# Up projection: weight rests formed by accumulating transfers, every second chunk rounded by a casting transfer

## Chip, cores and metric

The kernel runs on one core of a Trainium2 chip. The metric is device time in microseconds (us) for one execution. Before the change the median of two runs is 957.73 us (957.66 to 957.80).

## What is computed

The reference is one layer of a streaming encoder: a token mixer (pooling, latent attention and spatial gating, merged and projected), then a gated MLP with a causal convolution of three taps over positions. Sequence 512, model width 1024, MLP width 2816. The change lies in the MLP's up projection:

```python
def _conv_ffn(h, w_up, conv_w, conv_b, w_down):
    z = h @ w_up                      # (512 x 1024) @ (1024 x 5632)
    zp = jnp.pad(z, ((0, 0), (CONV_W - 1, 0), (0, 0)))
    zc = conv_b + conv_w[0] * zp[:, 0:S]
    for k in range(1, CONV_W):
        zc = zc + conv_w[k] * zp[:, k:k + S]
    val, gate = jnp.split(zc, 2, axis=-1)
    return (jax.nn.silu(gate) * val) @ w_down
```

All of it is float32.

## The kernel before

TensorE multiplies in the type fp32r, which holds fewer digits than float32. So each float32 operand is split: `hi` is the operand rounded to fp32r, `lo` is the rest, operand minus `hi`, again as fp32r. A product is then the sum of three: hi times lo, lo times hi, hi times hi.

The up projection's weight is laid out as 44 chunks `wup[m]` of 128 partitions x 1024 floats (512 KB). A chunk holds the weights of 128 output channels: eight blocks of 128 x 128, one for each block `k` of the model width. Chunks come in pairs: 2i is the value half and 2i+1 the gate half of the same 128 channels. The activations `h2_hi[k]`, `h2_lo[k]` (128 x 512) stay in SBUF through the stage. Chunks 0 to 5 are split earlier (`early_split`, `early_low`) and multiplied in two halves of 256 positions while the second half of `h2` is still made; chunks 6 to 43 (38 chunks, 19 pairs) go through `wsplit`, and these the change touches.

For one such chunk, before:

- `load` (lines 82 to 86): SP's queue issues a transfer from HBM to a tile `wup` (tag "raw", three buffers).
- L92: ScalarE rounds it to `wuph` (tag "whi", two buffers).
- L93: VectorE subtracts: `wupl` = `wup` - `wuph` (tag "wlo", two buffers).
- `mm_chunk` (lines 110 to 116): TensorE runs 24 matmuls of 512 columns into one PSUM bank `pzu`: sixteen with `wuph` (L113, L114), then eight with `wupl` (L116).
- L1384, L1387, L1391: ScalarE and twice VectorE make the convolution's three taps from `pzu`.

After each pair ScalarE takes Silu of the gate half (L1401), POOL multiplies the halves (L1402), ScalarE and VectorE split the product (L1405, L1406) for the down projection. In every second one of the first sixteen pairs, SP also loads two tiles `adar` of 256 KB (L848) for a later modulation row, which VectorE adds up (L850, L852). Near the end of the stage POOL scales the first down projection chunks (L1098).

The order on each engine's queue is written by the framework when the kernel is built; it follows the dependencies and its own estimate of times. On the chip each engine works its queue in that order, and an instruction that waits holds up those behind it. A buffer is written again only when its last reader is done. There are eight PSUM banks, so products of several chunks may be open at once.

Of the kernel before, what the change touches and what calls it, by code (L numbers as in the profile page):

```python
# [9 lines left out]
F32R = mybir.dt.float32r  # L10
I32 = mybir.dt.int32
AF = mybir.ActivationFunctionType
ALU = mybir.AluOpType
AX = mybir.AxisListType

P = 128
S = 512
D = 1024
# [32 lines left out]
def trunk(ctx: ExitStack, tc: tile.TileContext, A, out):  # L51
    nc = tc.nc
# [4 lines left out]
    wp = ctx.enter_context(tc.tile_pool(name="wp", bufs=2))  # L57
# [3 lines left out]
    def ps(name):  # L61
        return pp.tile([P, 512], F32, name=name, tag="ps")
# [16 lines left out]
    def f(ap):  # L79
        return ap.bitcast(F32)  # L80

    def load(src, n, name):
        raw = wp.tile([P, D], F32, name=name, tag="raw", bufs=3)
        with tc.issue_after(last_load[0]):
            nc.sync.dma_start(out=raw[:, :n], in_=src)
        return raw

    def wsplit(src, n, name):
        raw = load(src, n, name)
        hi = wp.tile([P, D], F32R, name=name + "h", tag="whi")  # L90
        lo = wp.tile([P, D], F32R, name=name + "l", tag="wlo")
        nc.scalar.copy(out=hi[:, :n], in_=raw[:, :n])  # L92
        ins = nc.vector.tensor_tensor(  # L93
            out=lo[:, :n], in0=raw[:, :n], in1=f(hi[:, :n]), op=ALU.subtract
        )
        last_lo[:] = [ins.ins]
        return hi, lo

    last_lo = []
# [10 lines left out]
    def mm_chunk(o, wh, wl, xh, xl):  # L110
        cs = [slice(k * P, (k + 1) * P) for k in range(KT)]
        for k, c in enumerate(cs):
            nc.tensor.matmul(o, wh[:, c], xl[k], start=k == 0, stop=False)  # L113
            nc.tensor.matmul(o, wh[:, c], xh[k], start=False, stop=False)  # L114
        for k, c in enumerate(cs):
            nc.tensor.matmul(o, wl[:, c], xh[k], start=False, stop=k == KT - 1)  # L116
# [56 lines left out]
    for t in range(TT):  # L173
        for n in range(2):
            x_load = (nc.scalar if t == 3 else nc.sync).dma_start(
                out=xs[t][n], in_=A["x"][t * P : (t + 1) * P, n * 512 : (n + 1) * 512]
# [401 lines left out]
    for t in range(TT):  # L578
# [3 lines left out]
        src = lat[t][:, 384:448].rearrange("p (a b) -> p a b", a=2)  # L582
        for dst, tab in ((tA, cosT), (tB, sinT)):
            nc.vector.tensor_tensor(
                out=dst[:, t, :].rearrange("p (a b) -> p a b", a=2), in0=src,
# [355 lines left out]
    for g in range(4):  # L941
        if g % 2 == 0:
            wh, wl = chunk(("wpool", g // 2))
        for mo in range(2):
            m = 2 * g + mo
# [81 lines left out]
    for n in range(2):  # L1027
        nc.gpsimd.affine_select(
            out=ws[n].rearrange("p (g t) -> p g t", g=4),
            in_=wsr[:, n * 512 : (n + 1) * 512].rearrange("p (g t) -> p g t", g=4),  # L1030
# [42 lines left out]
    for m in range(KT):  # L1073
        merge(2, m, sg_hi, sg_lo, th2.pop(m))
        if m < 6:
            raw = o_raw[2 + m // 2][m % 2]
# [5 lines left out]
            out=ml, in0=merged[m], scalar=0.5, in1=f(mh), op0=ALU.mult, op1=ALU.subtract  # L1082
# [241 lines left out]
    for t in range(TT):  # L1324
        x1[t] = [m_t(f"x1_{t}{n}") for n in range(2)]
        for n in range(2):
            nc.sync.dma_start(
                out=x1[t][n], in_=A["x"][t * P : (t + 1) * P, n * 512 : (n + 1) * 512]
# [13 lines left out]
    def up_early(ms, half, ks=range(KT)):  # L1342
        c = slice(half * 256, (half + 1) * 256)
        for m in ms:
            if half == 0 and m not in pzs:
                pzs[m] = ps("pzu")
        for k in ks:
            for m in ms:
                uh, ul, _ = early[m]
                w = slice((k % 4) * P, (k % 4 + 1) * P)  # L1350
                ins = mm3(
                    pzs[m][:, c], uh[k // 4][:, w], ul[k // 4][:, w],
                    h2_hi[k][:, c], h2_lo[k][:, c], k == 0, k == KT - 1,
                )
        return ins.ins
# [14 lines left out]
    for i in range(NP):  # L1370
        half = []
        for v in range(2):
            m = 2 * i + v
            if m < NE:
                if v == 0:
                    up_early((m, m + 1), 1)
                pz = pzs[m]
            else:
                uh, ul = wsplit(A["wup"][m], D, "wup")
                pz = ps("pzu")  # L1380
                mm_chunk(pz, uh, ul, h2_hi, h2_lo)
            cc = C_CONV + 4 * m
            t = pt_t("zc")
            nc.scalar.activation(  # L1384
                t, pz, AF.Identity, bias=cols[:, cc + 3 : cc + 4], scale=cols[:, cc + 2 : cc + 3]
            )
            nc.vector.scalar_tensor_tensor(  # L1387
                out=t[:, 1:512], in0=pz[:, 0:511], scalar=cols[:, cc + 1 : cc + 2],
                in1=t[:, 1:512], op0=ALU.mult, op1=ALU.add,
            )  # L1390
            nc.vector.scalar_tensor_tensor(  # L1391
                out=t[:, 2:512], in0=pz[:, 0:510], scalar=cols[:, cc : cc + 1],
                in1=t[:, 2:512], op0=ALU.mult, op1=ALU.add,
            )
            half.append(t)
        val, gate = half
        if i % 2 == 1 and i < 2 * KT:
            ada_piece(3, i // 2)
        if i == 2 * KT:
            gt_f = ada_rows(3, 1, "gtf")  # L1400
        nc.scalar.activation(gate, gate, AF.Silu)  # L1401
        nc.gpsimd.tensor_tensor(out=val, in0=val, in1=gate, op=ALU.mult)  # L1402
        ah = act_t(f"f{i}h")
        al = act_t(f"f{i}l")
        nc.scalar.copy(out=ah, in_=val)  # L1405
        nc.vector.tensor_tensor(out=al, in0=val, in1=f(ah), op=ALU.subtract)  # L1406
        a_hi.append(ah)
        a_lo.append(al)
# [150 lines left out]
```

## Time and profile before

| What | Value |
|---|---|
| Times of the two runs | 957.66 and 957.80 us |
| Span of the profiled execution, first to last instruction | 956.3 us |
| What lies outside the span, against 957.7 us | 1.4 us |
| TensorE busy | 942.2 us, 99% of the span |
| VectorE busy | 584.9 us, 61% |
| ScalarE busy | 380.3 us, 40% |
| POOL busy | 284.1 us, 30% |
| Data moved by transfers | 119.72 MB, 125 GB/s on average |
| The changed stage (chunks 6 to 43) | 621 to 829 us of the span |

The profile gives each engine's busy time, groups of instructions by source line with their mean time, who waited for whom, transfers with their time from issue to landing, and a table by stretches of the span. TensorE's matmuls overlap: one of 512 columns is shown as 0.39 us long, but the next starts 0.23 us later, so the pace is read from start times. Lines L1 to L93 keep their numbers in the changed kernel; later lines move up by 14.

### The profile page before, as it was taken

How to read it: one execution, taken by the hardware profiler on the slowest of the kernel's cores; microseconds unless marked ns; L12 is line 12 of the kernel's file. 1: busy time of each engine (PE TensorE's matmuls, PEld its weight loads, DVE VectorE, ACT ScalarE, POOL GpSimd, SP SyncE). 2: the span in 40 equal slices, each digit the busy share in tenths (PEclk: the TensorE clock that was granted, in tenths of full speed). 3: DMA queues.
4: the chain of work that ended last, by engine and by line, in shares of the span. 5: the costliest groups of instructions: out<-in, count | busy, mean ns of one | idle time of the engine just before them, and what ended most of it. 6: DMA issues, size and time to landing. Idle time of an engine off the chain costs nothing.

```text
span 956.3 us, 12108 instructions
## 1 busy us (share of the span) xinstructions
PE 942.2 (99%) x4556; PEld 795.5 (83%) x4556; DVE 584.9 (61%) x850; ACT 380.3 (40%) x623; POOL 284.1 (30%) x248
## 2 busy tenths in 40 slices
PE   7999999999999999999999999999999999999996
PEld 6988888888888888888888888988888888888885
DVE  7966767546786665567233589575565664623258
ACT  4575555533233322232322334644434444321121
POOL 4741121122440032202123713021111121756653
PEclk9999999999999999999999999999999999999999
DMA  9823202145436533554333540134334333432322
GB/s 324 318 72 100 62 31 83 45 132 154 135 111 216 181 118 109 181 182 141 124 110 114 165 162 24 60 118 131 110 119 140 115 119 102 129 114 88 91 86 89
DMA packets 46139, 119.72 MB, mean 125 GB/s; under 512 B 5504, under 2 KB 8960, under 8 KB 46080
## 3 DMA queue, kind: packets, MB, share of 16 engines
q1 hardware_dynamic: 45648, 118.39, 38.4%
q8 instruction: 36, 0.59, 0.2%
q10 hardware_dynamic: 432, 0.55, 0.2%
q14 instruction: 23, 0.19, 0.1%
HBM read 116.83 MB, written 2.10 MB: 124 GB/s over the span
## 4 chain that ended last, share of the span: by engine, by line
PE 86%; DMA 5%; DVE 5%; POOL 2%; issue 1%; ACT 1%; SPq 0%; POOLq 0%; DVEq 0%; ACTq 0%
PE pzu L114 7%; PE pzu L116 7%; PE pzu L113 7%; PE pg L113 4%; PE pg L114 4%; PE pg L116 4%; PE py L113 4%; PE py L114 4%; PE py L116 4%; PE pyd L1132 3%; PE pyd L1129 3%; PE pyd L1131 3%; DMA ada<-in_ada1p 2%; PE pu L114 2%; PE pu L113 2%; PE pu L974 2%
## 5 line engine op out<-in xcount | busy, mean ns | idle before, releaser
L93 DVE TENSOR_TENSOR wupl<-wup,wuph 128x1024 fp32r<-128x1024 f32 x38 | 47.8, 1257 | 71.8 <-PE pzu L116 45.9
L1098 POOL TENSOR_TENSOR d<-d,gtfb 128x512 f32<-128x512 f32 x44 | 73.7, 1697 | 38.1 <-DMA d<-in_wdn 36.5
L1402 POOL TENSOR_TENSOR zc<-zc 128x512 f32<-128x512 f32 x22 | 29.7, 1350 | 173.1 <-ACT zc L1401 130.8
L1103 DVE TENSOR_TENSOR dl<-d,dh 128x1024 fp32r<-128x1024 f32 x18 | 27.8, 1542 | 57.0 <-PE pyd L1129 51.9
L92 ACT CAST wuph<-wup 128x1024 fp32r<-128x1024 f32 x38 | 39.9, 1049 | 46.8 <-PE pzu L114 46.8
L417 POOL TENSOR_TENSOR mg<-mg,th 128x512 f32<-128x512 f32 x16 | 31.3, 1959 | 86.4 <-DVE th L414 86.4
L92 ACT CAST wbh<-wb 128x1024 fp32r<-128x1024 f32 x24 | 25.2, 1052 | 74.0 <-PE py L114 55.3
L852 DVE SCALAR_TENSOR_TENSOR ada<-adar,cact,ada 128x512 f32<-128x512 f32 x56 | 49.1, 907 | 1.8 <-DMA adar<-in_ada 1.8
L93 DVE TENSOR_TENSOR wgl<-wg,wgh 128x1024 fp32r<-128x1024 f32 x22 | 29.6, 1343 | 29.7 <-PE pg L116 14.9
L1102 ACT CAST dh<-d 128x1024 fp32r<-128x1024 f32 x18 | 18.9, 1052 | 62.5 <-PE pyd L1132 33.2
L1384 ACT ACTIVATE zc<-pzu,cols 128x512 f32<-128x512 f32 x44 | 34.1, 778 | 21.8 <-PE pzu L116 17.4
L93 DVE TENSOR_TENSOR wbl<-wb,wbh 128x1024 fp32r<-128x1024 f32 x24 | 30.6, 1275 | 14.9 <-ACT wbh L92 6.5
L771 POOL TENSOR_SCALAR pe<-pe,mx 128x128 f32<-128x128 f32 (+3 forms) x32 | 17.0, 533 | 69.3 <-DVE mx L770 52.4
L1387 DVE SCALAR_TENSOR_TENSOR zc<-pzu,cols,zc 128x511 f32<-128x511 f32 x44 | 32.6, 744 | 4.2 <-ACT zc L1384 4.2
L92 ACT CAST wgh<-wg 128x1024 fp32r<-128x1024 f32 x22 | 23.3, 1058 | 25.6 <-PE pg L114 19.8
L1391 DVE SCALAR_TENSOR_TENSOR zc<-pzu,cols,zc 128x510 f32<-128x510 f32 x44 | 32.6, 745 | 0.8
L414 DVE SCALAR_TENSOR_TENSOR th<-th,py 128x512 f32<-128x512 f32 x16 | 11.0, 687 | 35.6 <-PE py L116 35.6
L1401 ACT ACTIVATE zc<-zc 128x512 f32<-128x512 f32 x22 | 13.9, 631 | 40.5 <-DVE zc L1391 40.4
L905 POOL TENSOR_TENSOR asum<-apad 128x527 f32<-128x527 f32 x8 | 12.3, 1544 | 54.6 <-ACT apad L900 28.0
L296 DVE SCALAR_TENSOR_TENSOR acc<-ada,cact,acc 128x256 f32<-128x256 f32 (+1 forms) x29 | 27.4, 944 | 1.2 <-DMA ada<-in_ada1p 0.3
L1077 POOL TENSOR_TENSOR oraw<-oraw,gttb 128x512 f32<-128x512 f32 x6 | 10.5, 1775 | 47.3 <-DMA oraw<-in_wo 47.3
L1098 POOL TENSOR_TENSOR o<-o,gttb 128x512 f32<-128x512 f32 x10 | 17.4, 1757 | 13.5 <-DMA o<-in_wo 7.7
(1473 smaller groups left out, 3088.4 us busy)
## 6 DMA issues: line engine op xcount, KB each, us to landing
wup<-in_wup SPq DMA_DIRECT2D x44, 512.0 KB, 3.6
adar<-in_ada SPq DMA_DIRECT2D x64, 256.0 KB, 4.1
wb<-in_wb SPq DMA_DIRECT2D x24, 512.0 KB, 3.6
wg<-in_wg SPq DMA_DIRECT2D x22, 512.0 KB, 3.6
d<-in_wdn SPq DMA_DIRECT2D x22, 512.0 KB, 3.6
ada<-in_ada1p SPq DMA_DIRECT2D x24, 256.0 KB, 4.9
wa<-in_wa SPq DMA_DIRECT2D x8, 512.0 KB, 3.6
wsg<-in_wsg SPq DMA_DIRECT2D x8, 512.0 KB, 3.6
```

Source lines behind the costliest of these rows:

```text
L92: nc.scalar.copy(out=hi[:, :n], in_=raw[:, :n])
L93: ins = nc.vector.tensor_tensor(out=lo[:, :n], in0=raw[:, :n], in1=f(hi[:, :n]), op=ALU.subtract)
L113: nc.tensor.matmul(o, wh[:, c], xl[k], start=k == 0, stop=False)
L114: nc.tensor.matmul(o, wh[:, c], xh[k], start=False, stop=False)
L116: nc.tensor.matmul(o, wl[:, c], xh[k], start=False, stop=k == KT - 1)
L417: nc.gpsimd.tensor_tensor(out=merged[m], in0=merged[m], in1=th, op=ALU.add)
L852: nc.vector.scalar_tensor_tensor(out=acc[n], in0=src, scalar=cact[:, k : k + 1], in1=acc[n], op0=ALU.mult, op1=ALU.add,)
L1098: nc.gpsimd.tensor_tensor(out=halves[n], in0=halves[n], in1=gt[n], op=ALU.mult)
L1384: nc.scalar.activation(t, pz, AF.Identity, bias=cols[:, cc + 3 : cc + 4], scale=cols[:, cc + 2 : cc + 3])
L1387: nc.vector.scalar_tensor_tensor(out=t[:, 1:512], in0=pz[:, 0:511], scalar=cols[:, cc + 1 : cc + 2], in1=t[:, 1:512], op0=ALU.mult, op1=AL ...
L1391: nc.vector.scalar_tensor_tensor(out=t[:, 2:512], in0=pz[:, 0:510], scalar=cols[:, cc : cc + 1], in1=t[:, 2:512], op0=ALU.mult, op1=ALU.add,)
L1402: nc.gpsimd.tensor_tensor(out=val, in0=val, in1=gate, op=ALU.mult)
```

## The change

Chunks 6 to 43 go through a new function, `dsplit`. An odd chunk is loaded by SP and rounded by ScalarE as before. An even chunk is not loaded to a raw tile: POOL issues a transfer that reads HBM and writes `wuph` as fp32r. Then, for every chunk, ScalarE writes minus `wuph` to `wupl`, and POOL issues a transfer that adds the unrounded chunk to what stands in `wupl`: an even chunk from HBM, which is so read a second time, an odd one from its raw tile in SBUF. VectorE's subtraction is gone. In the rows of the changed kernel L103 is the casting transfer, L107 the rounding of an odd chunk, L109 the negation, L110 an accumulating transfer.

```diff
+    def dsplit(src, n, name, cast):
+        hi = wp.tile([P, D], F32R, name=name + "h", tag="whi")
+        lo = wp.tile([P, D], F32R, name=name + "l", tag="wlo")
+        if cast:
+            nc.gpsimd.dma_start(out=hi[:, :n], in_=src)
+            rest = src
+        else:
+            raw = load(src, n, name)
+            nc.scalar.copy(out=hi[:, :n], in_=raw[:, :n])
+            rest = raw[:, :n]
+        nc.scalar.activation(lo[:, :n], f(hi[:, :n]), AF.Copy, scale=-1.0)
+        nc.gpsimd.dma_start(out=lo[:, :n], in_=rest, accum_op=ALU.add)
+        return hi, lo
...
-                uh, ul = wsplit(A["wup"][m], D, "wup")
+                uh, ul = dsplit(A["wup"][m], D, "wup", m % 2 == 0)
                 pz = ps("pzu")
                 mm_chunk(pz, uh, ul, h2_hi, h2_lo)
```

The queues are written anew with it. **POOL, in the middle of the stage, before** (`zc` are the two halves of a pair's taps):

```order
L1402 TENSOR_TENSOR zc_5746<-zc_5746,zc_5781 128x512
L1402 TENSOR_TENSOR zc_5828<-zc_5828,zc_5863 128x512
L1402 TENSOR_TENSOR zc_5904<-zc_5904,zc_5939 128x512
L1402 TENSOR_TENSOR zc_5986<-zc_5986,zc_6021 128x512
L1402 TENSOR_TENSOR zc_6062<-zc_6062,zc_6097 128x512
```

**POOL, the same place, with the change** (in square brackets the semaphores that the instruction waits for; DMASW are those of POOL's own transfers, DMAHW those of SP's):

```order
L103 DMA wuph_5873<-in_wup 128x1024 [waits DMASW3_49,PE_49]
L110 DMA wupl_5874<-in_wup 128x1024 [waits DMASW4_49,PE_49,Activation_49]
L110 DMA wupl_5908<-wup_5909 128x1024 [waits DMASW5_49,DMAHW7_49,PE_49,Activation_49]
L1416 TENSOR_TENSOR zc_5827<-zc_5827,zc_5863 128x512 [waits Activation_49,Pool_49]
L103 DMA wuph_5955<-in_wup 128x1024 [waits DMASW6_49,PE_49]
L110 DMA wupl_5956<-in_wup 128x1024 [waits DMASW7_49,PE_49,Activation_49]
L110 DMA wupl_5990<-wup_5991 128x1024 [waits DMASW0_49,DMAHW2_49,PE_49,Activation_49]
L1416 TENSOR_TENSOR zc_5903<-zc_5903,zc_5939 128x512 [waits DMAHW3_49,Activation_49]
```

Where POOL had one multiplication a pair, it now has in each pair, in this order, a casting transfer, two accumulating ones, and the multiplication of the pair that TensorE finished last.

**ScalarE, the same place, with the change**, two pairs apart by one row of L1419:

```order
L107 CAST wuph_5907<-wup_5909 128x1024
L1398 ACTIVATE zc_5827<-pzu_5802,cols_73 128x512
L109 ACTIVATE wupl_5874<-wuph_5873 128x1024
L1398 ACTIVATE zc_5863<-pzu_5838,cols_73 128x512
L109 ACTIVATE wupl_5908<-wuph_5907 128x1024
L1415 ACTIVATE zc_5863<-zc_5863 128x512
L1419 CAST f4h_5869<-zc_5827 128x512
```

Per pair one rounding is gone and two negations (L109) have come; the negations for the next pair stand between the taps (L1398) of the pair that TensorE is finishing.

**TensorE, the end of one chunk's hi part, before:**

```order
L114 MATMUL pzu_5756<-h2T7h_4802,wuph_5752 128x512
L116 MATMUL pzu_5756<-h2T0h_4795,wupl_5753 128x512
L116 MATMUL pzu_5756<-h2T1h_4796,wupl_5753 128x512
L116 MATMUL pzu_5756<-h2T2h_4797,wupl_5753 128x512
L116 MATMUL pzu_5756<-h2T3h_4798,wupl_5753 128x512
L116 MATMUL pzu_5756<-h2T4h_4799,wupl_5753 128x512
L116 MATMUL pzu_5756<-h2T5h_4800,wupl_5753 128x512
```

**TensorE with the change**, where the hi part of a pair's odd chunk (`pzu_5914`) ends:

```order
L128 MATMUL pzu_5914<-h2T7h_4802,wuph_5907 128x512
L130 MATMUL pzu_5878<-h2T0h_4795,wupl_5874 128x512
L130 MATMUL pzu_5878<-h2T1h_4796,wupl_5874 128x512
L130 MATMUL pzu_5878<-h2T2h_4797,wupl_5874 128x512
L130 MATMUL pzu_5878<-h2T3h_4798,wupl_5874 128x512
L130 MATMUL pzu_5878<-h2T4h_4799,wupl_5874 128x512
L130 MATMUL pzu_5878<-h2T5h_4800,wupl_5874 128x512
L130 MATMUL pzu_5878<-h2T6h_4801,wupl_5874 128x512
L130 MATMUL pzu_5878<-h2T7h_4802,wupl_5874 128x512
L130 MATMUL pzu_5914<-h2T0h_4795,wupl_5908 128x512
```

Before, a chunk's eight lo matmuls followed its own sixteen hi matmuls. Now a pair runs as: even chunk's sixteen hi, odd chunk's sixteen hi, even chunk's eight lo, odd chunk's eight lo.

## The prediction

> **What bounds the kernel now.** I read the page's first part, then the table by stretches over the changed stage, then the list of waits, then the chain of waits. The page:
>
> ```profile
> PE 942.2 (99%) x4556; PEld 795.5 (83%) x4556; DVE 584.9 (61%) x850; ACT 380.3 (40%) x623; POOL 284.1 (30%) x248
> ```
>
> TensorE (PE) is busy for nearly the whole span. That is an average, so the stretches of the stage come next (columns: stretch, its length, busy time of TensorE, its weight loads, VectorE, ScalarE, POOL; then granted clock, share of the 16 DMA engines, GB/s):
>
> ```profile
> 620.00:666.00 46.00, 46.00 (x210) 38.31 (x209) 32.18 (x41) 23.05 (x31) 9.01 (x6) 1.00 0.40 126
> 666.00:710.00 44.00, 44.00 (x196) 36.45 (x195) 26.25 (x34) 19.02 (x24) 5.17 (x4) 1.00 0.38 120
> 710.00:753.00 43.00, 43.00 (x191) 35.61 (x191) 25.25 (x32) 19.02 (x24) 5.17 (x4) 1.00 0.38 123
> 753.00:797.00 44.00, 44.00 (x196) 36.37 (x195) 26.47 (x33) 20.19 (x26) 9.13 (x6) 1.00 0.39 120
> ```
>
> TensorE fills each of them to the last hundredth, at full granted clock; VectorE is near 60%, ScalarE under half, POOL at an eighth to a fifth, the transfers at 0.4. The whole run's list of TensorE's waits says the same from the other side:
>
> ```profile
> PE lat L480 <- DMA x<-in_x: 5.5, 1, 5.5
> PE pth L1247 <- ACT xr L1234: 0.6, 1, 0.6
> PE pqn L106 <- ACT wqk2h L120: 0.3, 1, 0.3
> PE sc L758 <- DVE PTl L121: 0.2, 1, 0.2
> ```
>
> No row names the stage's matmuls (`pzu`), and VectorE has TensorE waiting for 0.2 us in all. The chain of waits in the stage is TensorE alone; its lo parts give the pace:
>
> ```profile
> 635.86 1.81 PE pzu L116 x8
> ...
> 690.25 1.81 PE pzu L116 x8
> ```
>
> Ten chunks in 54.39 us: 5.44 us a chunk, 10.88 us a pair, 0.2266 us a matmul. So sixteen hi matmuls take 3.63 us and eight lo ones 1.81 us. Whatever the change takes from VectorE, this stage can get no shorter than that. The question is only whether weights come late.
>
> **The change, part by part.** The operations that go or move:
>
> ```profile
> L93 DVE TENSOR_TENSOR wupl<-wup,wuph 128x1024 fp32r<-128x1024 f32 x38 | 47.8, 1257 | 71.8 <-PE pzu L116 45.9 <-ACT wuph L92 24.4 <-ACT adah L864 1.6
> L92 ACT CAST wuph<-wup 128x1024 fp32r<-128x1024 f32 x38 | 39.9, 1049 | 46.8 <-PE pzu L114 46.8
> L1384 ACT ACTIVATE zc<-pzu,cols 128x512 f32<-128x512 f32 x44 | 34.1, 778 | 21.8 <-PE pzu L116 17.4 <-PE pzu L108 4.4
> L1402 POOL TENSOR_TENSOR zc<-zc 128x512 f32<-128x512 f32 x21 | 28.4, 1352 | 173.1 <-ACT zc L1401 130.8 <-PE pzu L108 22.6 <-PE pzu L114 10.1
> ```
>
> *Removed:* 38 subtractions, 47.8 us of VectorE, beside TensorE's work: worth nothing to the end. Also 19 roundings on ScalarE (1.05 us each) and 19 plain loads on SP.
>
> *Added on ScalarE:* 38 negations of 128x1024. The trace has none; the rounding has the same engine and shape, so 1.05 us each, net 19 x 1.05 = 20 us over a stage of 208 us in which ScalarE is idle more than half. Hidden as work. But the negation of an even chunk waits for a casting transfer to land, and behind it in ScalarE's queue stand the taps of the odd chunk before, Silu, and the split of the product.
>
> *Added on POOL:* 57 transfers, three a pair. The issue is not in the trace. Bounds: SP issues a load in 0.42 us, POOL needs 1.35 us for a pass of its own (L1402); I take 0.9, their middle. POOL is otherwise idle enough. Behind a waiting transfer stand the pair's multiplication and the next casting transfer.
>
> *The transfers themselves.* What the trace shows of them:
>
> ```profile
> wup<-in_wup SPq DMA_DIRECT2D x44, 512.0 KB, 3.6
> L848 SPq DMA_DIRECT2D adar<-in_ada x16: 328/424/426, 613.8 to 759.5; - x16
> ```
>
> A plain chunk of 524,288 bytes lands 3.6 us after issue. The stretch 666 to 710 moves 120 GB/s at a share of 0.38, so 316 GB/s when all engines are busy, and a chunk takes 1.66 us of engine time; the other 1.94 us are the way there and back. The casting transfer moves the same bytes: I give it 1.66 + 1.94. The accumulating transfer is the disputed price. Lower bound: it costs what a load costs, 1.66 us of engine time. Upper bound: it is a whole landing more than a load, 3.6 + 1.66 = 5.26. It must bring in the old contents beside the new, so twice the bytes go in: 2 x 1.66 = 3.32 us. I take that, which is also near the middle.
>
> The Trainium skill (Collectives: The Full Stack, section "The bandwidth ceiling: the fold count and why AG ≠ RS ≠ AR") says that an add inside a transfer needs two source reads, which halves its rate in measured collectives, 62.28 against 32.35 GB/s. No run here shows it yet. By that rule the sum below stands; if an add moved at a copy's rate, the time would be that of the first rival.
>
> *Where it comes to wait.* A negation needs its even chunk's casting transfer landed; the accumulating transfers need the negations; and the next casting transfer stands behind them in POOL's queue and, if the DMA engines serve POOL's transfers in the order of issue, in theirs. So from one cast's landing to the next there is a loop: negation 1.05, signal to POOL 0.14, issue 0.9, even chunk's add 3.32, odd chunk's add 3.32, next cast 1.66, way back 1.94. Sum 12.33 us, where TensorE needs 10.88. The signal is from these rows (646.60 to 646.74):
>
> ```profile
> 645.97 0.63 ACT L1401 ACTIVATE zc<-zc 128x512 f32<-128x512 f32 x1 [2.04 <-DVE zc L1391]
> 646.74 1.29 POOL L1402 TENSOR_TENSOR zc<-zc 128x512 f32<-128x512 f32 x1 [9.11 <-ACT zc L1401]
> ```
>
> Other loads use the same engines: one raw chunk a pair (1.66 us) and sixteen `adar` tiles of half a chunk over sixteen pairs (0.83 us a pair), 2.49 us. The loop's transfers hold the engines for 8.3 of 12.33 us, so up to 0.67 x 2.49 = 1.7 us of it would lengthen the loop. SP loads ahead into three raw buffers and need not meet them; I take half, 0.84. The loop is then 13.17 us, 2.29 more than TensorE's pair, and over the 18 pairs after the first that is 41.2 us.
>
> *The first pair.* Its buffers come free at 616.6, when ScalarE made its first rounding, and TensorE begins it at 621.16:
>
> ```profile
> 616.64 1.04 ACT L92 CAST wuph<-wup 128x1024 fp32r<-128x1024 f32 x1
> 621.16 0.40 PE L113 MATMUL pzu<-h2T0l,wuph 128*128 128x512 f32 x1
> 621.32 1.93 POOL L1402 TENSOR_TENSOR zc<-zc 128x512 f32<-128x512 f32 x1 [22.60 <-PE pzu L108]
> ```
>
> The cast lands at 616.64 + 0.9 + 3.6 = 621.1, just in time. The negation ends at 622.2, but POOL's first multiplication stands ahead of the add, to 623.25. Issue to 624.15; the even chunk's rest lands 3.32 + 1.94 later, at 629.4. TensorE wants it two hi parts after its start, at 628.4: 1.0 us late. The odd one lands at 632.7, wanted at 629.4 + 1.81 = 631.2: 1.5 us. Together 2.5.
>
> *What helps.* TensorE's new order puts both hi parts first, so that a rest is wanted 7.25 us after its pair begins instead of 3.63. Without it each even chunk's rest would be wanted 3.63 us sooner. The loop is not shortened by it. The PE work itself is unchanged, and the down projection behind keeps its buffers and order.
>
> *Sum.* Profiled execution: span 956.3 + 1.4 outside = 957.7, which is the median of the two runs (957.73). 957.7 + 41.2 + 2.5 = 1001 us.
>
> **The rivals.**
>
> 1. *The adds are hidden: no change.* This ends on the other side. At a copy's 1.66 us for each add, the loop is 12.33 - 3.32 + 0.84 = 9.85 us, under 10.88; the first pair's rest lands at 627.75, before 628.4. Time 958. For it: the transfers' share of 0.4 leaves room, and three casts or adds and a load at copy rate are 6.6 of 10.88 us. Against it: the old contents must be read too. It decides up to 1.66 + (10.88 - 9.85) / 2 = 2.2 us for an add; up to some 2.7 us the loss stays within 19 us, the 2% that a measurement of this kernel can tell from no change.
>
> 2. *The adds are much dearer.* At 5.26 us each the loop is 12.33 + 3.88 + 0.84 = 17.05, 6.2 us a pair over TensorE's, 111 us, and 6 us in the first pair: 1075 us. For it: reading, adding and writing back might not overlap inside an engine. Against it: nothing in this trace; it has no such transfer.
>
> 3. *POOL's issue is dear.* There is a second loop: the odd chunk's last lo matmul, signal 0.14, its tap 0.78, the next odd chunk's negation 1.05, signal 0.14, issue 0.9, add and way back 5.26, eight lo matmuls 1.81. It is 10.1 us, 0.8 short of binding. Issue at 2 us would make it 11.2, and the first loop 14.3, hence 1021 us. POOL's own pass of 1.35 us speaks against 2 us. It lies within the forecast's and the second rival's times and gets no chance of its own.
>
> 4. *Faster.* VectorE's lists would have to hide waits of TensorE. They show 0.2 us in the whole run; the best is 957.5.
>
> Does the change do what it says? The queues show that the subtractions are gone and the three transfers a pair are there.
>
> **How the numbers follow.** Forecast (loop between 11.9 and 15.5 us, 977 to 1040): 0.45. Hidden or nearly: 0.29. Dearer, over 1040: 0.25. Faster: 0.01. So faster 0.01, within 2% 0.29, slower 0.70. The range goes from no loss, 957, to an add of nearly 5.3 us with other loads fully in the way (17.05 + 0.84 = 17.9 us, so 126 us, and 6 in the first pair), 1090; above lies perhaps 0.12. The forecast's own range is 977 to 1040.
>
> **What would show it.** Right: TensorE idle ahead of its lo matmuls (L130) or hi matmuls (L127), released by POOL's transfers, about 2 us a pair; even chunks' casts landing well behind issue; the DMA share near 0.9 in the stage; VectorE some 48 us less busy. Adds that land within 4 us of issue and TensorE without a gap would speak for the first rival; adds of 7 us and more for the second; POOL busy 2 us for an issue for the third. The forecast is wrong if the waits are elsewhere, say on SP's raw loads, or if the adds of a pair run side by side instead of in a row.

## The result and the profile after

The changed kernel takes 979.15 us, the median of two runs (977.53 and 980.77), against 957.73 us: a ratio of 1.0223, 95% interval 1.0207 to 1.0240. The direction was forecast, and the mechanism is found in the pairs. The size was not: +21 us where +43 was predicted. The profiled execution took 980.77 us, with a span of 979.1.

First the page and the stretches of the stage, to be held beside those of before (columns as there):

```profile
PE 952.4 (97%) x4556; PEld 796.4 (81%) x4556; DVE 549.8 (56%) x812; ACT 399.2 (41%) x642; POOL 320.8 (33%) x305
```

```profile
620.00:666.00 46.00, 44.26 (x201) 35.88 (x200) 23.09 (x29) 25.68 (x34) 17.04 (x18) 1.00 0.83 195
666.00:710.00 44.00, 42.86 (x184) 34.04 (x184) 19.15 (x24) 22.32 (x28) 14.26 (x16) 1.00 0.86 202
...
797.00:830.00 33.00, 29.89 (x129) 23.50 (x128) 9.50 (x13) 14.56 (x18) 12.70 (x14) 1.00 0.74 160
830.00:860.00 30.00, 28.03 (x109) 22.06 (x108) 10.83 (x13) 11.51 (x14) 15.81 (x12) 0.89 0.58 159
```

TensorE has gaps now, and the transfers' share has gone from 0.40 to 0.83 and 0.86. The last two rows lose more than the first two. TensorE's waits over the whole span name who is late (total us, times, longest):

```profile
PE pzu L130 <- DMA wupl<-in_wup: 8.5, 5, 3.1
...
PE pzu L130 <- DMA wupl<-wup: 1.5, 4, 0.4
```

What is new against the list of before are lo matmuls (L130) waiting for adds. None waits for a cast (L127). Now how long POOL's three kinds of transfer take from issue to landing, in the median:

```profile
wuph<-in_wup POOLq DMA_DIRECT2D x19, 512.0 KB, 6.0
wupl<-in_wup POOLq DMA_DIRECT2D x19, 512.0 KB, 5.6
wupl<-wup POOLq DMA_DIRECT2D x19, 512.0 KB, 6.5
```

The loop of the prediction can be read off one long pair of the timeline (start, duration, and in brackets the idle time before and who ended it):

```profile
654.57 1.06 ACT L109 ACTIVATE wupl<-wuph 128x1024 fp32r<-128x1024 f32 x1 [1.01 <-DMA wuph<-in_wup]
655.93 0.86 POOL L110 DMA_DIRECT2D wupl<-in_wup  x1 [6.77 <-ACT wupl L109]
663.50 0.50 PE L130 MATMUL pzu<-h2T0h,wupl 128*128 128x512 f32 x1 [1.27 <-DMA wupl<-in_wup]
665.97 0.50 PE L130 MATMUL pzu<-h2T0h,wupl 128*128 128x512 f32 x1 [0.37 <-DMA wupl<-wup]
667.26 1.06 ACT L109 ACTIVATE wupl<-wuph 128x1024 fp32r<-128x1024 f32 x1 [0.84 <-DMA wuph<-in_wup]
```

From a negation to its add's issue 1.36 us; to the even add's landing 7.57; to the odd add's 2.47; to the next cast's, which lets the next negation start, 1.29. Sum 12.69 us, where TensorE needs 10.88.

The pairs are not alike. Their starts, from the first matmul of each, are 10.88 to 11.3 us apart in most pairs, 11.9 and 12.1 in two, and 13.05 to 13.23 in three of the seven ahead of which SP has just issued loads of two modulation tiles. The first of the stage and the last but one:

```profile
621.73 0.40 PE L127 MATMUL pzu<-h2T0l,wuph 128*128 128x512 f32 x1
817.78 0.47 PE L127 MATMUL pzu<-h2T0l,wuph 128*128 128x512 f32 x1
```

Between them lie 17 pairs: 196.05 us against 17 x 10.88 = 184.96. In the kernel before the same 17 pairs took 1.0 us more than 184.96 too (185.97, from 621.16 to 807.13), mostly because four matmuls of the modulation row (L870, now L884) stand among them. So the pairs lose **+10.1**. The last two pairs end at 850.3: 32.5 us against 21.76. But the new order has put seven matmuls of the down projection, 1.6 us, ahead of their last eight, so they lose **+9.2**. The stage begins 0.6 us later than before (621.16); that is there from its first chunk on (603.49 against 602.91), before the first casting transfer of these pairs at 616.8. In the down projection behind the stage nothing is lost.

The rest of the 22.8 us by which the span has grown is lost after the computation. POOL's last pass, before and with the change:

```profile
952.74 0.96 POOL L1446 TENSOR_TENSOR out<-out,lnfb 128x256 f32<-128x256 f32 x1 [0.94 <-ACT out L1445]
```

```profile
972.58 0.96 POOL L1460 TENSOR_TENSOR out<-out,lnfb 128x256 f32<-128x256 f32 x1 [0.94 <-ACT out L1459]
```

From its end to the end of the span pass 2.6 us before (953.70 to 956.3) and 5.5 with the change (973.54 to 979.1): **+2.9**. In the runs below this goes with the number of POOL's transfers: 2.7 us with 19 of them (casts alone, odd chunks alone), 4.0 with 38 (adds alone, even chunks alone), 5.0 with 51 (the last two pairs the old way), and 5.5 with 57, whatever else was changed. What the program does in that time no row here shows. So the 22.8 us are 0.6 + 10.1 + 9.2 + 2.9. The end of the stage has its own look:

```profile
815.69 0.33 SPq L85 DMA_DIRECT2D d<-in_wdn  x1
820.23 2.54 POOL L1112 TENSOR_TENSOR d<-d,gtfb 128x512 f32<-128x512 f32 x2 [7.95 <-DMA d<-in_wdn]
822.72 0.86 POOL L110 DMA_DIRECT2D wupl<-in_wup  x1
828.40 0.50 PE L130 MATMUL pzu<-h2T0h,wupl 128*128 128x512 f32 x1 [3.10 <-DMA wupl<-in_wup]
```

POOL's queue has the scaling of a down projection chunk `d` (L1112) ahead of the pair's adds. The scaling waits 7.95 us for the load of `d`. The load is late because SP waits for a raw tile that an odd chunk's add still reads (SP's own waits, 800 to 860 us):

```profile
SPq L85 <- DMA wupl<-wup: 51.3, 4, 14.8
```

So the add is issued at 822.72, and TensorE waits 3.10 us for it. In the last pair the same happens again, with a wait of 1.97 us, and behind each of the two waits TensorE runs slower for a while (last section).

In the experiments below, what pairs lose is counted in the same way: against the kernel before, and without the matmuls that a new order moved in or out of the stretch. The expectations still have 11 and 10.8 us where this count gives 10.1 and 9.2.

### The profile page after: what moved, and what is told of

Read it like the earlier page. It is cut to its first block, busy times and chain, and to the rows that moved or that the text cites. A ratio compares the mean times of both kernels' runs of the same rounds, so it can differ in the third digit from the quotient of the medians.

```text
span 979.1 us, 12213 instructions
## 1 busy us (share of the span) xinstructions
PE 952.4 (97%) x4556; PEld 796.4 (81%) x4556; DVE 549.8 (56%) x812; ACT 399.2 (41%) x642; POOL 320.8 (33%) x305
## 3 DMA queue, kind: packets, MB, share of 16 engines
q0 software_dynamic: 8208, 29.89, 14.3%
## 4 chain that ended last, share of the span: by engine, by line
PE 80%; DMA 10%; issue 4%; DVE 3%; POOL 1%; ACT 1%; POOLq 0%; SPq 0%; ACTq 0%
DMA wupl<-wup 5%; PE py L127 4%; PE py L128 4%; PE py L130 4%; PE pg L127 4%; PE pg L128 4%; PE pg L130 4%; PE pzu L130 3%; PE pyd L1145 3%; PE pyd L1146 3%; PE pyd L1143 3%; PE pzu L128 3%; PE pzu L127 3%; DMA wuph<-in_wup 3%; PE pu L127 1%
## 5 line engine op out<-in xcount | busy, mean ns | idle before, releaser
L1112 POOL TENSOR_TENSOR d<-d,gtfb 128x512 f32<-128x512 f32 x44 | 69.8, 1611 | 55.9 <-DMA d<-in_wdn 55.9
L866 DVE SCALAR_TENSOR_TENSOR ada<-adar,cact,ada 128x512 f32<-128x512 f32 x56 | 54.0, 1004 | 7.2 <-DMA adar<-in_ada 7.2
L92 ACT CAST wbh<-wb 128x1024 fp32r<-128x1024 f32 x24 | 25.3, 1054 | 74.0 <-PE py L128 55.3
L110 POOL DMA_DIRECT2D wupl<-in_wup x19 | 16.5, 867 | 105.6 <-ACT wupl L109 105.6
L1398 ACT ACTIVATE zc<-pzu,cols 128x512 f32<-128x512 f32 x44 | 33.8, 772 | 32.5 <-PE pzu L130 28.1
L109 ACT ACTIVATE wupl<-wuph 128x1024 fp32r<-128x1024 f32 x38 | 40.0, 1054 | 14.3 <-DMA wuph<-in_wup 14.3
L92 ACT CAST wgh<-wg 128x1024 fp32r<-128x1024 f32 x22 | 23.3, 1059 | 25.6 <-PE pg L128 19.9
L107 ACT CAST wuph<-wup 128x1024 fp32r<-128x1024 f32 x19 | 20.0, 1050 | 28.8 <-PE pzu L128 28.5
L130 PE MATMUL pzu<-h2T0h,wupl 128*128 128x512 f32 x38 | 17.1, 449 | 10.1 <-DMA wupl<-in_wup 8.5
L1091 POOL TENSOR_TENSOR oraw<-oraw,gttb 128x512 f32<-128x512 f32 x6 | 10.5, 1773 | 47.5 <-DMA oraw<-in_wo 47.5
```

What stands on the lines that cost most here:

```text
L109: nc.scalar.activation(lo[:, :n], f(hi[:, :n]), AF.Copy, scale=-1.0)
L866: nc.vector.scalar_tensor_tensor(out=acc[n], in0=src, scalar=cact[:, k : k + 1], in1=acc[n], op0=ALU.mult, op1=ALU.add,)
L1112: nc.gpsimd.tensor_tensor(out=halves[n], in0=halves[n], in1=gt[n], op=ALU.mult)
L1398: nc.scalar.activation(t, pz, AF.Identity, bias=cols[:, cc + 3 : cc + 4], scale=cols[:, cc + 2 : cc + 3])
```

## The experiments

**The prices by themselves.** A kernel that leaves out the whole computation and only moves weight chunks: each kind of transfer alone, then four in a row, then adds beside loads.

```diff
+            nc.sync.dma_start(out=load[i], in_=W[m])
...
+            nc.gpsimd.dma_start(out=plain[i], in_=W[m])
...
+            nc.gpsimd.dma_start(out=cast[i], in_=W[m])
...
+            nc.gpsimd.dma_start(out=hadd[i], in_=W[m], accum_op=ALU.add)
...
+        nc.gpsimd.dma_start(out=sadd[i], in_=plain[i], accum_op=ALU.add)
...
+    for kind in ("load", "plain", "cast", "hadd", "sadd"):
+        for rep in range(3):
```

> Leaves out the whole computation; it only issues transfers of 512 KB chunks: plain loads from SP, plain, casting and accumulating transfers from POOL, three of each one at a time, then four of each in a row, then adds beside SP's loads, then add, add, cast in a row twice. Theory 1 (the loop is made of the transfers' own time on the engines, and my add was too dear): a cast costs about a load's 1.7 us in a row, an add between 2.2 and 2.8 us, from the changed kernel's shortest landing, 5.3 us, less 0.87 for the issue and 1.94 for the way. Rival (an add is as dear as predicted and the loss is small for another reason): adds in a row 3.3 us apart.

The timeline: a small copy (`seen`) starts when its transfer has landed. L92 and L114 are a cast alone, L95 and L114 an add from HBM alone, L126 four in a row.

```profile
25.11 0.53 POOL L92 DMA_DIRECT2D cast<-in_wup  x1
28.78 0.18 POOL L114 COPY seen<-cast 128x1 f32<-128x1 f32 x1 [3.14 <-DMA cast<-in_wup]
...
36.87 0.90 POOL L95 DMA_DIRECT2D hadd<-in_wup  x1
42.23 0.18 POOL L114 COPY seen<-hadd 128x1 f32<-128x1 f32 x1 [4.46 <-DMA hadd<-in_wup]
...
73.41 0.18 POOL L126 COPY seen<-load 128x1 f32<-128x1 f32 x1 [1.07 <-DMA load<-in_wup]
74.67 0.18 POOL L126 COPY seen<-load 128x1 f32<-128x1 f32 x1 [1.08 <-DMA load<-in_wup]
...
100.16 0.18 POOL L126 COPY seen<-hadd 128x1 f32<-128x1 f32 x1 [2.44 <-DMA hadd<-in_wup]
102.60 0.18 POOL L126 COPY seen<-hadd 128x1 f32<-128x1 f32 x1 [2.26 <-DMA hadd<-in_wup]
```

From issue to landing a cast takes 3.7 to 3.9 us and an add from HBM 5.4 to 5.6; an add from SBUF takes 4.6 (54.08 to 58.68). In a row loads land 1.26 us apart, casts 1.24 to 1.5, adds 2.44 to 2.65 from either memory. **An add holds the engines twice as long as a copy, and a copy 1.25 us, not 1.66.** Add, add and cast issued one behind another were served in that order. Four adds beside four of SP's loads took 17.96 us to the last landing, four alone 12.96: each load costs the adds its whole 1.25 us. With these prices the loop, left to itself, is 1.36 + 5.4 + 2.5 + 1.25 = 10.5 us, just under TensorE's 10.88, and a raw load and two modulation tiles that get into its way bring it to 13.0.

**The end: the scaling behind the last add.**

```diff
-        nc.gpsimd.dma_start(out=lo[:, :n], in_=rest, accum_op=ALU.add)
+        ins = nc.gpsimd.dma_start(out=lo[:, :n], in_=rest, accum_op=ALU.add)
+        last_add[:] = [ins.ins]
...
-            for n in range(2):
-                nc.gpsimd.tensor_tensor(out=halves[n], in0=halves[n], in1=gt[n], op=ALU.mult)
+            with ExitStack() as order:
+                if last_add:
+                    order.enter_context(tc.issue_after(last_add[0]))
+                for n in range(2):
+                    nc.gpsimd.tensor_tensor(out=halves[n], in0=halves[n], in1=gt[n], op=ALU.mult)
```

> The changed kernel, with POOL's scaling of the down projection's chunks ordered behind the stage's last accumulating transfer. Theory 1: the last two pairs lose 10.8 us because a scaling stands ahead of the pair's adds in POOL's queue, and waits for a load that waits for a raw buffer held by the add of an earlier pair; with the order changed the last two pairs take 11 to 12 us each in place of 16.2, and the time falls by 7 to 11 us, to some 970. Rival (the end is slow because the down projection's loads crowd the transfer engines): no change, 977 to 981.

Measured 974.86 us (973.98 to 976.23), ratio 1.0182 [1.0165, 1.0199]. The last two pairs take 11.5 and 11.0 us and lose 0.7 instead of 9.2. The first 17 pairs lose 8.0. But 4.3 us come back as a loss behind the stage, where TensorE now waits for the scaled chunks (`PE pyd L1150 <- ACT dh L1121: 2.4`) and is slower behind that wait. The gain, 4.3 us between the medians, is smaller than the 7 to 11 that I had expected. So the scaling's place in POOL's queue does hold up the last pairs, and moving it alone saves about half of the 9.2 us.

**Without the modulation loads.** Fourteen of the sixteen tiles `adar` are not loaded; VectorE's adds read another tile, so the kernel no longer computes the same.

```diff
-            src = pt_t(f"adar{n}")
-            nc.sync.dma_start(out=src, in_=A["ada2"][idx, k, :, n * 512 : (n + 1) * 512])
+            if idx == 3 and k:
+                src = x1[0][n]
+            else:
+                src = pt_t(f"adar{n}")
+                nc.sync.dma_start(out=src, in_=A["ada2"][idx, k, :, n * 512 : (n + 1) * 512])
```

> The changed kernel, with fourteen of the sixteen loads of adar in the stage left out (seven of eight modulation pieces are taken from other data in SBUF, which changes the last modulation row). Theory 1 (transfers take turns on the engines): every second pair, which has two such loads beside it and takes 12 to 13.2 us, falls to about 11; the first seventeen pairs lose 2 to 4 us in place of 11; time 968 to 973. Rival (the loop is POOL's queue and the waits in it): pairs keep their lengths, time 977 to 981.

Measured 975.87 us (973.53 to 977.53), ratio 1.0186 [1.0168, 1.0204]. No pair of 13 us is left (one of 12.13, in which the modulation row's four matmuls stand; the rest 10.9 to 11.7). The first 17 pairs lose 6.0 us instead of 10.1; the end still loses 9.5. So these loads cost 4 us of the 10. I had expected 2 to 4 us to be left; more is.

**The pair's multiplication on VectorE**, which takes it out from between the adds and the next cast on POOL.

```diff
-        nc.gpsimd.tensor_tensor(out=val, in0=val, in1=gate, op=ALU.mult)
+        nc.vector.tensor_tensor(out=val, in0=val, in1=gate, op=ALU.mult)
```

> The changed kernel, with the product of a pair's halves (22 multiplications of 128x512) made by VectorE in place of POOL, so that the next casting transfer no longer stands behind Silu and that product and is issued over 1 us earlier. Theory 1 (transfers take turns on the engines, so an earlier issue only waits longer there): the first seventeen pairs still lose 8 to 12 us; the end unchanged; 976 to 981. Rival (POOL's queue is the loop): each stalled pair is 1.3 us shorter, the first seventeen pairs lose 0 to 3 us, time 968 to 972.

Measured 977.32 us (974.82 to 978.16), ratio 1.0199 [1.0182, 1.0216]; the first 17 pairs lose 9.1. The cast can be issued sooner, but it lands later after its issue, 6.4 us in the median instead of 6.0: it stands behind the adds in the transfers' own order. POOL's arithmetic is not what binds.

**The last two pairs the old way.**

```diff
-                uh, ul = dsplit(A["wup"][m], D, "wup", m % 2 == 0)
+                uh, ul = wsplit(A["wup"][m], D, "wup") if m >= 40 else dsplit(A["wup"][m], D, "wup", m % 2 == 0)
```

> The changed kernel, but the stage's last four chunks are split the old way (a plain load, ScalarE's rounding, VectorE's subtraction). Theory 1 (the end is lost because POOL's scaling of down chunks stands ahead of adds and waits for a buffer that an add holds): no add is left behind a scaling and no scaling is put off, so the last two pairs run at 10.9 to 11.2 us each, nothing is given back in the down projection, and only the 7 to 11 us of the pairs before stay: 965 to 970. Rival (the end is slow because of crowding by the down projection's loads, or because a stall anywhere lowers TensorE's clock): 973 or more.

Measured 970.53 us (968.74 to 972.96), ratio 1.0135 [1.0115, 1.0156]. The end loses nothing, but the pairs before it lose 12.5 us, with four pairs of 12.8 to 13.3, so that the time is just above the 965 to 970 that I had expected. The queues were written anew; that more pairs met other loads would explain the 2.4 us more, and no run shows it. It bears out that the end's loss is of the end; its sum with the rest is not simply additive.

**Adds alone: no cast.** Every chunk is loaded and rounded as an odd one.

```diff
-                uh, ul = dsplit(A["wup"][m], D, "wup", m % 2 == 0)
+                uh, ul = dsplit(A["wup"][m], D, "wup", False)
```

> The adds alone: every chunk is loaded by SP and rounded by ScalarE as before the change, then negated by ScalarE and completed by an add from its raw tile in SBUF; no casting transfer. Theory 1 (the loop goes from a cast's landing over the adds to the next cast): without casts there is no loop, the pairs before the last two take 10.9 to 11.1 us and lose 0 to 3 us in all; a scaling still stands ahead of the last add, so up to 6 us at the end: 958 to 967. Rival (adds crowd the engines or come too late by themselves): the pairs lose as much as in the changed kernel, 7 to 11 us, and the time is 968 to 980.

Measured 1007.8 us (1006.94 to 1009.56), ratio 1.0525 [1.0509, 1.0541]: far slower than the change itself. My theory had this one run without loss, and as I had put it, it falls: taking the cast out of the loop does not open it. The timeline shows what took the cast's place:

```profile
656.71 0.88 POOL L110 DMA_DIRECT2D wupl<-wup  x1 [7.95 <-PE pzu L128]
661.17 0.33 SPq L85 DMA_DIRECT2D wup<-in_wup  x1
665.89 1.05 ACT L107 CAST wuph<-wup 128x1024 fp32r<-128x1024 f32 x1 [6.39 <-DMA wup<-in_wup]
668.04 1.05 ACT L109 ACTIVATE wupl<-wuph 128x1024 fp32r<-128x1024 f32 x1
669.38 0.88 POOL L110 DMA_DIRECT2D wupl<-wup  x1 [8.28 <-ACT wupl L109]
```

An add reads its raw tile until it lands, 4.46 us after issue. Only then can SP load into that tile (the load goes out at 661.17, with the landing), and the load needs 4.7 us more. ScalarE's queue has the rounding of this new chunk (665.89) ahead of the negation of the chunk before it (668.04), so that negation waits for the load too. One turn, from add to add two chunks on, is 12.67 us. So here the loop goes through the raw tile, which VectorE's subtraction used to free early. This is read from the timeline; no run gave the raw tiles another buffer.

**Casts alone: no adds.** Even chunks are cast, and loaded as well for VectorE's subtraction.

```diff
         if cast:
             nc.gpsimd.dma_start(out=hi[:, :n], in_=src)
-            rest = src
+            raw = load(src, n, name)
...
-        nc.scalar.activation(lo[:, :n], f(hi[:, :n]), AF.Copy, scale=-1.0)
-        nc.gpsimd.dma_start(out=lo[:, :n], in_=rest, accum_op=ALU.add)
+        nc.vector.tensor_tensor(
+            out=lo[:, :n], in0=raw[:, :n], in1=f(hi[:, :n]), op=ALU.subtract
+        )
```

> The casting transfers alone: an even chunk's hi part comes from a casting transfer, and the chunk is loaded by SP besides; every rest is VectorE's subtraction as before the change; no negation and no add. Theory 1: a cast lands under 4 us after issue, has over 5 us, and no add stands ahead of it: no loss, 957 to 960. Rival (casting transfers come late by themselves, since POOL issues them behind its multiplication): each even chunk late by about 1 us, 970 to 980.

Measured 957.92 us (957.04 to 958.94), ratio 1.0002 [0.9993, 1.0011]. TensorE has no gap. The casts' landing is the line to see:

```profile
wuph<-in_wup POOLq DMA_DIRECT2D x19, 512.0 KB, 3.9
```

3.9 us here, 6.0 in the changed kernel: the 2.1 us between are the adds ahead of them.

**Three hi buffers**, so that a cast need not wait for the pair's hi matmuls. To make room, a pool of five other buffers has four, and one small tile shares another's buffers.

```diff
-    pd = ctx.enter_context(tc.tile_pool(name="pd", bufs=5))
+    pd = ctx.enter_context(tc.tile_pool(name="pd", bufs=4))
...
-        hi = wp.tile([P, D], F32R, name=name + "h", tag="whi")
+        hi = wp.tile([P, D], F32R, name=name + "h", tag="whi", bufs=3)
```

> The changed kernel with three buffers in place of two for the hi parts (one buffer less of another pool pays for it). The queues are written anew: in most pairs the next cast now stands between the even and the odd chunk's add, so that the loop holds one add instead of two. Theory 1 (the loop is negation, adds, cast and their landing): the loop falls by an add's 2.5 us, under TensorE's pair, the first seventeen pairs lose 0 to 4 us in place of 11, the end remains: 966 to 973. Rival (the transfer engines are simply too busy, at a share of 0.83 to 0.95): the pairs still lose 8 to 11 us: 976 to 981.

Measured 981.52 us (979.83 to 981.90), ratio 1.0243 [1.0226, 1.0260]. The total hides several things, which the stretches and TensorE's timeline take apart:

```profile
666.00:710.00 44.00, 44.00 (x195) 36.42 (x195) 16.81 (x23) 21.79 (x27) 14.26 (x16) 1.00 0.89 209
710.00:753.00 43.00, 43.00 (x191) 35.61 (x191) 15.46 (x22) 22.40 (x27) 12.14 (x14) 1.00 0.89 204
```

```profile
780.70 0.79 PE L130 MATMUL pzu<-h2T0h,wupl 128*128 128x512 f32 x1 [7.16 <-DMA wupl<-in_wup]
```

From 666 to 753 us TensorE has no gap at all, with all the transfers of the change and a share of 0.89, higher than in the changed kernel. So the amount of transfer was not the bound there; the order in which one waits for the other was. What opened the loop is not what I had expected, the cast between a pair's two adds; that order came out in four pairs only. From 655 to 776 us the cast still stands behind both adds, as here:

```profile
691.89 0.86 POOL L110 DMA_DIRECT2D wupl<-in_wup  x1 [4.56 <-ACT wupl L109]
695.51 0.86 POOL L110 DMA_DIRECT2D wupl<-wup  x1 [2.76 <-ACT wupl L109]
698.07 0.60 POOL L103 DMA_DIRECT2D wuph<-in_wup  x1
```

But the first cast of the stage is issued at 551.8, so each later one is a pair ahead of its place in the changed kernel, and the next negation no longer waits for it: in this stretch ScalarE waits for no cast, where its negations in the changed kernel waited 14.3 us for casts in all. The stage also begins at 623.45 us instead of 621.73; the smaller pool may be why, which no run shows. And the new order on TensorE has an even chunk's lo part stand hard behind the odd one's at 773.5, when its add had been issued only at 772.80: one wait of 7.16 us, and more around it.

**Even chunks alone the new way; odd chunks alone.**

```diff
-                uh, ul = dsplit(A["wup"][m], D, "wup", m % 2 == 0)
+                uh, ul = wsplit(A["wup"][m], D, "wup") if m % 2 else dsplit(A["wup"][m], D, "wup", True)
```

```diff
-                uh, ul = dsplit(A["wup"][m], D, "wup", m % 2 == 0)
+                uh, ul = dsplit(A["wup"][m], D, "wup", False) if m % 2 else wsplit(A["wup"][m], D, "wup")
```

> Only even chunks go the new way (cast, negation, add from HBM); odd chunks are rounded and subtracted as before. Loop theory, with the prices measured alone: negation 1.05, signal 0.3, add landing 5.4 after issue, cast behind it 1.25: 8.0 us a pair, with a raw load and two modulation loads in the way 10.5, under 10.88. So the first 17 pairs of the stage run at 10.9, no raw tile is held by an add, and the time is 957.7 to 963. Rival (adds are slow because the transfers crowd each other, and each add costs its share): half of the loss stays, 966 to 970.

> Only odd chunks go the new way (load, rounding, negation, add from the raw tile); even chunks as before. Loop theory: no cast waits behind an add, so there is no loop of transfers; the first 17 pairs run at 10.9. A raw tile is still held by its add, and the scaling for the down projection may still stand ahead of adds at the end (up to 5 us): 958 to 964. Rival (each add costs its share): 966 to 970.

Even alone: 969.46 us (969.30 to 970.60), ratio 1.0124 [1.0109, 1.0139]; the first 17 pairs lose 7.6 us, the last two nothing, and TensorE waits 2.8 more at the start of the down projection, with slower matmuls behind it. The time is in the rival's range, not in mine. ScalarE, POOL and TensorE in one long pair:

```profile
644.72 0.89 POOL L110 DMA_DIRECT2D wupl<-in_wup  x1 [5.73 <-ACT wupl L109]
653.11 0.50 PE L130 MATMUL pzu<-h2T0h,wupl 128*128 128x512 f32 x1 [0.94 <-DMA wupl<-in_wup]
654.49 1.06 ACT L109 ACTIVATE wupl<-wuph 128x1024 fp32r<-128x1024 f32 x1 [3.04 <-DMA wuph<-in_wup]
```

SP had issued a raw load at 644.46 and two modulation tiles at 644.84. The add lands some 8.4 us after issue: 5.4 + 1.25 + 1.25 is 7.9. The cast, behind it, lets the next negation start 1.4 us later. With the negation at 643.37 a turn is 11.1 us, 0.6 more than the 10.5 that I had with all these loads in the way, and the add itself is late for TensorE. So the loop is there with one add as well; I had priced its worst turn a little too low and had not seen that it comes so often.

Odd alone: 965.84 us (965.68 to 966.01), ratio 1.0084 [1.0067, 1.0100]. That is between my range and the rival's. TensorE has no gap from 620 to 753 us. There is no cast behind an add here, and no loss in those pairs, as the loop theory has it: nineteen adds as such cost TensorE nothing there. What is lost is nearly all lost at one place:

```profile
776.87 0.50 PE L884 MATMUL pgt<-adal,onesr 128*128 128x512 f32 x1 [1.74 <-POOL adal L879]
777.19 0.89 POOL L110 DMA_DIRECT2D wupl<-wup  x1 [0.37 <-ACT wupl L109]
```

Two passes that POOL makes for the modulation row (L879) now stand before and behind an add in its queue, and TensorE waits 3.6 us for them (the second at 779.42, 1.82), after 0.9 us for an add and with a lower clock behind.

**The odd chunk's add from HBM too**, so that its raw tile comes free after the rounding.

```diff
-            rest = raw[:, :n]
+            rest = src
```

> As the changed kernel, but the odd chunk's add reads HBM too, so its raw tile comes free after the rounding. Theory for the last two pairs: the scaling on POOL stood ahead of the adds and waited for a load whose raw tile an add still held; now the load is early, the last two pairs lose under 4 us of their 10.8, and the first 17 pairs keep their 11: 970 to 974. Rival (the order of POOL's queue alone makes the end late): 977 to 981.

Measured 973.04 us (972.60 to 974.10), ratio 1.0161 [1.0146, 1.0176]. The first 17 pairs lose 10.0 us, as in the changed kernel; the last two lose 1.7 instead of 9.2. SP's waits at the end (800 to 860 us) no longer name an add:

```profile
SPq L85 <- ACT wuph L107: 32.0, 3, 11.1
```

The scalings wait 0.2 and 0.4 us for their loads at 807 and 819 us, where the changed kernel waited 7.95. So without the held raw tile most of the end's loss is gone, as it is with the scaling behind the adds: as far as the two runs show, the loss needs both. This run does not part them wholly, since POOL's queue was written anew and now has one add of each pair ahead of the scaling.

**The negation of even chunks twice over.** The second write repeats the first.

```diff
-        nc.scalar.activation(lo[:, :n], f(hi[:, :n]), AF.Copy, scale=-1.0)
+        for _ in range(2 if cast else 1):
+            nc.scalar.activation(lo[:, :n], f(hi[:, :n]), AF.Copy, scale=-1.0)
```

> As the changed kernel, but the negation of each even chunk is done twice over (the second write repeats the first). ScalarE is idle half of the stage. Loop theory: the second negation lies on the loop from cast to negation to adds to cast, and a tap stands between the two in ScalarE's queue, 1.05 + 0.65 = 1.7 us a pair with at most 0.4 of slack: the first 17 pairs lose 22 to 29 us more than in the changed kernel, 1000 to 1009. Rival (the transfers' crowding sets the pace, ScalarE is hidden): 977 to 983.

Measured 994.15 us (993.02 to 996.77), ratio 1.0383 [1.0367, 1.0400]. ScalarE is idle for half of the stage, and yet its 20 us of extra work (19 x 1.05) cost the first 17 pairs 18.3 us more than in the changed kernel (214.4 against 196.05). That is 1.08 a pair, about the second negation alone; I had 22 to 29 in all, because I had counted the tap between the two as well. The turn reads (L110 is the negation here, L111 the add, L131 the lo matmul):

```profile
656.75 1.06 ACT L110 ACTIVATE wupl<-wuph 128x1024 fp32r<-128x1024 f32 x1 [1.00 <-DMA wuph<-in_wup]
659.72 0.86 POOL L111 DMA_DIRECT2D wupl<-in_wup  x1 [8.85 <-ACT wupl L110]
665.39 0.50 PE L131 MATMUL pzu<-h2T0h,wupl 128*128 128x512 f32 x1 [0.50 <-DMA wupl<-in_wup]
667.96 0.50 PE L131 MATMUL pzu<-h2T0h,wupl 128*128 128x512 f32 x1 [0.46 <-DMA wupl<-wup]
669.23 1.06 ACT L110 ACTIVATE wupl<-wuph 128x1024 fp32r<-128x1024 f32 x1 [0.91 <-DMA wuph<-in_wup]
```

2.97 from the first negation to the add's issue, 5.67 to its landing, 2.57 to the odd add's, 1.27 to the cast's: 12.48 us, and the transfers' prices are near those measured alone (5.4, 2.5 and 1.25). The loop is shown: what is put on it comes out as time, nearly whole.

## Why the prediction was right in kind and wrong in size

*What bounds the kernel, and where the wait appears:* right. TensorE was the bound; it now waits ahead of L130 for POOL's transfers, casts land 6.0 us after issue, and the share stands at 0.83 to 0.86.

*The loop:* right as a mechanism, from cast to negation to two adds to cast. The doubled negation shows it, term by term. The three hi buffers show it from the other side: with the casts a pair ahead, TensorE had no gap from 666 to 753 us. The run with adds alone showed that it is not the only loop: with no cast a raw tile closes a like one.

*The price of a transfer:* this step failed. The term "a chunk takes 1.66 us of engine time", which stands five times over in the loop of 12.33 us, was worked out as bytes over the rate at full share, 316 GB/s, from a stretch whose share was 0.38. Measured in a row, a chunk takes 1.25 us. The share counts more than the engines' need, so this quotient gives a rate that is too low. The factor two for an add was right: 2.5 against 1.25. The Trainium skill (Collectives: The Full Stack, section "The bandwidth ceiling: the fold count and why AG ≠ RS ≠ AR") has an add at half rate because it reads two sources; the ratio in the trace agrees, 2.44 to 2.65 us against 1.25, so about 2.0, and no run here shows the reason. The two adds and the cast are 6.25 us, not 8.30. That alone takes the loop from 12.33 to 10.28, below TensorE's 10.88.

*The other loads:* half of them, 0.84 us in each pair, was a mean where no mean holds. Pairs that run at TensorE's pace win nothing back for those that don't. The loop by itself is 10.5; the turn quoted above, which meets other loads, is 12.69, and the longest pairs take 13.05 to 13.23. The 17 pairs lose 10.1 us, 0.6 a pair, instead of 41.2 in 18, 2.29 a pair. With the price put right and the mean kept (0.84 x 1.25 / 1.66 = 0.63), the loop would be 10.9 us and the sum about 958, so this way of adding up would then have missed the 10 us. The modulation tiles are 4 us of them. That the rest are raw loads fits the prices, but no run here took those away by themselves.

*The first pair:* 2.5 us predicted, none measured: it takes 10.91 us, as it did before. With adds at 2.5 instead of 3.32 its rests come in time.

*The end:* "the down projection behind keeps its buffers and order" was wrong, and cost 9.2 us that the sum did not hold. The buffers were the same, but an add keeps its source tile until it lands, so the loads of `d` came late; and in POOL's queue the scaling stood ahead of the adds. I had listed POOL's scaling in the kernel's description and not followed the new queue as far as the end. A further 2.9 us, from the last pass to the end of the span, go with POOL's 57 transfers, and the sum had no term for them. So the errors partly hid each other: some 34 us too much in the pairs, 12 too little behind them.

*The rivals.* "The adds are hidden" gave up to some 2.7 us for an add as the price at which the loss stays within 2%; the add is 2.5, and the pairs alone lost 10.1 us, 1.1%. It was the end of the stage and the end of the program that took the total over 2%. So it was luck that the measured time fell into the forecast's 977 to 1040: the loop as corrected gives no loss in the mean, and more than half of the 21 us come from terms that the sum did not have. "Much dearer" falls with 2.5. POOL's issue is in the mean 0.87 to 0.89 us for an add and 0.64 for a cast, against the 0.9 that was assumed. VectorE is less busy by 35.1 us, not by 48, and that buys nothing, as predicted; part of what is missing is its modulation adds, 907 ns each before and 1004 after. Why, no run here tells.

None of the versions beats the kernel before; casts alone come out the same.

## What to carry to other kernels

An accumulating transfer spares VectorE's work and is dear in time: it holds its target and its source until it lands, so follow what waits for both, on every queue and to the end of the stage, before counting the vector work that it saves. Where a loop of waits comes out close to the bound, price its parts alone and look at single pairs: the excess of the long ones is lost and the slack of the short ones is not gained. Do not take a transfer's time from bytes over rate over share; take it from the distance of landings in a row. And follow the loss to the last row: 57 transfers of POOL went with 2.9 us after the work was done.

## What was not expected of the hardware

After some waits TensorE is slower for a while. Behind those of 3.10 and of 1.97 us at the end of the changed kernel the granted clock reads:

```profile
831.00:834.00 3.00, 3.00 (x9) 2.38 (x10) 1.50 (x2) 1.80 (x2) 0.00 (x0) 0.61 0.73 216
...
843.00:847.00 4.00, 3.63 (x9) 2.86 (x10) 0.00 (x0) 0.00 (x0) 0.00 (x0) 0.57 0.54 105
```

Matmuls of 512 columns there start 0.42 us apart instead of 0.227 (831.50, then 831.92). The first slow stretch begins 1.5 us after TensorE has resumed, the second (0.43 us apart from 843.82 on) almost at once, and each lasts about 3.4 us. So a wait costs more than its row: the pair that holds the 3.10 us lost 5.3. Behind the waits of 1.06 to 1.27 us in this kernel nothing of the kind is seen. The length of the wait alone does not decide it, though: in the run with three hi buffers a wait of 2.27 us, to 847.43, has none behind it (granted clock 1.00 from 847 to 851). What does, no run here tells.

The idle column also reads low by itself. The pair from 654.69 to 667.92 took 2.35 us too long, and its two waits add up to 1.64: a matmul's modelled end covers 0.17 us of each gap, and the first matmul behind a wait takes 0.11 us longer (0.50 instead of 0.39). That makes 2.2 of the 2.35.
